# Two strips of one projection that take their weight groups in turns

## The chip, the cores and the metric

The kernel runs on one core of one Trainium2 chip. The metric is the device time of one execution in microseconds (us); the kernel before takes 2448.28 us, the median of three runs. Five engines work side by side, each through its own list of instructions in order: TensorE (PE, matrix products; PEld are its weight loads), VectorE (DVE), ScalarE (ACT), GpSimd (POOL) and SyncE (SP, which issues most of the DMAs). An instruction that must wait for another engine holds up all that stand behind it in its own list.

## The reference

Two layers work on 256 tokens of 2048 features, in float32. The even layer matters here:

```
h = rms_norm(x, g)
p = h @ w_in                      # 2048 x 4384: u | r k v | three low ranks
y_s5 = s5_mixer(u, ...)           # complex state space, 64 groups of 16 channels
y_rw = rwkv7_mixer(r, k, v, ...)  # 16 heads, a 64 x 64 state each
x = x + rms_norm(concat(y_s5, y_rw) @ w_out, g2)
x = x + rms_norm(swiglu(rms_norm(x, g3)), g4)
```

The odd layer has a gated linear recurrence in place of the two mixers, and a swiglu of the same size.

## The kernel before

**The weight stream.** Features lie on partitions, tokens on the free axis. Every projection is cut into *strips* of up to 512 output columns. A strip is fed by *groups* of weights: one group is 256 rows of the weights, [128, 2, 512] in float32. A group comes by DMA (`raw`), is split into a high part (`hi`, on ScalarE) and a low part (`lo`, on VectorE, raw minus hi), and TensorE then makes 24 products with it: 2 tiles of rows, 4 tiles of columns, and three products for each (hi by x high, hi by x low, lo by x high; lines 513 to 515). `raw`, `hi` and `lo` have three buffers each, so a group can only be split when the third group before it has been used up. Four accumulators of a strip fill two PSUM banks; two strips can have theirs at a time. In the profile the accumulators are `psw`.

**The order.** `Lanes` (lines 173 to 207) decides in what order instructions are written: the weight stream goes on, and work beside it stands in generators, one at a time in a lane, each of which is taken a step further when a clock that the program itself keeps says that its inputs are there. On the chip that order is fixed. What TensorE does for the two mixers thus stands between the groups of the stream, at places that were chosen when the program was written out.

**The opening.** The first two strips are the two halves of u, `w_u[0]` and `w_u[1]`, 8 groups each. The first one also makes its own input: `h_before(g)` scales and splits two more tiles of x (`hh` on ScalarE, line 136; `hl` on VectorE, line 131) ahead of a group, `h_behind(g)` squares tiles (`sqs`) for the norm. The sums of squares give 1 / rms (`rs`, a chain of nine small VectorE instructions, then `rstdp` on TensorE, then `rstd`). When a strip is through, `u_evac` multiplies its PSUM by that and copies it by quarters into `U` (16 copies on ScalarE, 16 on VectorE).

**S5.** Its parameters are made on VectorE (`params`), then GpSimd and VectorE make matrices for eight pieces e = 0 to 7 (`wb`, `cb`), TensorE transposes and multiplies them (`tp`, `kt`, `tm`), and `main(e)` goes: `bu` (TensorE, from `U` and `wts`), about 14 VectorE instructions with two scans, `py` (TensorE). Pieces 0 to 3 need the first half of u, 4 to 7 the second.

**RWKV.** After u come `w_lr` and eight strips of r, k, v (`w_p`), whose evacuation `elem(p)` makes the inputs of four sets of heads. When S5 is done, `solve(hf)` runs for hf = 0 to 3, one after the other in one lane: `qp` on TensorE, copies, two trips through DRAM, and 31 steps on GpSimd. `chunks(hf)`, in another lane, follows each with transposes (`vt`, `bt`, `at`), products, and four chunks of the state (`st`, `sa`, `yp`), then `norm` (`yc` on VectorE, `tp`, `gp` on TensorE, `yl`, `yrf`).

**The end of it.** The output projection takes the S5 half first (`w_eo[0]`), then two strips of the RWKV half up to their third group. There all mixer lanes are drained (`L.drain("el", "qa", "qb", "gn")`, line 1577). The fourth groups, `e0.go(3)` and `e1.go(3)`, need the last head set, split into `yrh` and `yrl`. From there on, through both swiglus and the odd layer, nearly all of the time is weight stream.

Of the kernel before, what the change touches and what calls it, by code (L numbers as in the profile page):

```python
# [19 lines left out]
T = 256  # L20
D = 2048
# [46 lines left out]
def build(tc, a, out):  # L68
# [10 lines left out]
    # An estimate of when each engine is free and each tile is written, in us: it decides the  # L79
    # order in which instructions are emitted, nothing else.  # L80
# [44 lines left out]
    def pick(n, *aps, bias=1.0):  # L125
        """VectorE or Pool, whichever is through with n elements first; VectorE never waits."""
        v, t = max(clk["V"], L.now), dep(*aps)
        return V if t < v + 0.2 and v + bias + 0.00104 * n < max(clk["G"], L.now, t) + 0.0021 * n else G
# [44 lines left out]
    class Lanes:  # L173
        """The order of emission: what runs beside the weight stream is generators, one at a
        time in each lane, that yield how many us their next step should wait for. `now`
        counts TensorE's time."""
# [41 lines left out]
    with ctx:  # L218
# [17 lines left out]
        # ---------------------------------------------------------------- small helpers  # L236
# [38 lines left out]
        def rsqrt(o, x, shape, nm):  # L275
            """o = x ** -0.5 for a few columns: an integer first guess, two Newton steps (the
            first with its constants fitted to the guess)."""
# [40 lines left out]
        def together(*gs):  # L318
            """The steps of several generators, in turns."""
            gs = list(gs)  # L320
            while gs:
                for g in list(gs):
                    if next(g, 0) == 0:
                        gs.remove(g)
                    else:
                        yield

        # rstd of each token, in every partition (in PSUM), from the sums of squares
        def keep_warm(n):
            """TensorE's clock halves when it idles for some us: products of ones that nobody  # L330
            reads, where it would wait."""
# [22 lines left out]
        class Ssq:  # L354
            """Sums over the features of the squares, plus D eps: a column for each half of the
            tokens. Squares add up by pairs of tiles before TensorE sums over the partitions."""
# [15 lines left out]
            def place(self, sums=1):  # L372
                """Where the next pair of squares goes; the first ones are the sums."""
# [18 lines left out]
        # ---------------------------------------------------------------- weight stream  # L392
        RAW, HL = [3], [3]   # how far ahead
        groups = []          # (dram, k group), in the order of use
# [3 lines left out]
        # the tiles of the stream; a second pool takes every fourth one after the even layer  # L398
# [40 lines left out]
        unread = []          # of each strip, whether its PSUM has still to be read  # L439

        class Banks:
            """Four tiles of PSUM in two banks, which are read on their own; the last tile may have
            one more bank for itself."""
# [16 lines left out]
        class Strip:  # L460
            """w [kg, 128, 2, W] in DRAM; x(k): (hi, lo) [128, T] of a k tile; the n tiles
            accumulate side by side in two PSUM banks. evac(ps) may return a generator; `lazy`
            says that it reads PSUM there. hook(g) comes before a group; mid makes the tiles of x:
            mid[0](g) comes before the split of a group, mid[1](g) after it."""
# [62 lines left out]
            def tail(self):  # L527
                """The last two groups, one PSUM bank after the other."""
# [25 lines left out]

        W4 = [P] * 4

        def of2(z):
            """k -> (hi, lo) of a tensor kept as two slots of eight tiles, hi and lo."""
# [5 lines left out]
        # the whole weight stream, in its order  # L564
# [10 lines left out]

        def plan_ffn(l):
# [3 lines left out]
        plan(*w_u, w_lr, *w_p, *w_glu, *w_eo[0], (w_eo[1][0], range(3)), (w_eo[1][1], range(3)),  # L580
# [9 lines left out]
        # ================================================================ even layer  # L590
        even = ExitStack()
        with even:
# [11 lines left out]
            # ---- S5: parameters  # L604
# [36 lines left out]
            def wrap_small(o, x, n):  # L641
                """As wrap, for up to 64 turns; two steps on ScalarE."""
# [10 lines left out]
            def params():  # L653
                """A = exp(lam dt), its powers (apw: of 4 down to 0), gamma = (A - 1) / lam, and
                the size and the angle of A^4."""
# [37 lines left out]
                def powers():  # L693
                    for s, w, t in ((3, 1, 2), (2, 2, 0)):
                        # A^2 from A, then A^3 and A^4 from A^2
# [51 lines left out]
            # ---- the norm of x: its scale goes into the split, 1 / rms into what is read of PSUM  # L747
# [53 lines left out]
            def normed(ps):  # L801
                """What a strip has in PSUM, times 1 / rms of each token."""
# [14 lines left out]
            # ---- S5, four pairs of groups at a time: q says which 32 rows of a 128-row tile, s  # L817
            # which four tiles. Blocks of four steps: row (lag, channel), column (pair, block).
# [25 lines left out]
            def s5_gen():  # L844
# [14 lines left out]
                def prep_b(e):  # L859
                    """B scaled, times the powers of A: the matrix of the input, by lag; the real  # L860
                    part of C A^j, and minus its imaginary part."""
# [7 lines left out]
                def prep_w(e):  # L869
# [12 lines left out]
                    # the response at lags 0 to 3, as a block of a Toeplitz matrix  # L882
# [974 lines left out]
def pack(inp):  # L1857
    f = np.ascontiguousarray
    g = {k: np.asarray(v) for k, v in inp.items()}
    o = {}  # L1860
# [82 lines left out]
```

## Time and profile before

| | |
|---|---|
| median of three runs | 2448.28 us (2446.85, 2448.28, 2451.95) |
| the profiled execution, its span from first to last instruction | 2446.8 us (no other time is given for it) |
| TensorE busy | 2373.5 us, 97% |
| VectorE, ScalarE, GpSimd busy | 1469.4, 1181.0, 411.8 us |
| granted TensorE clock, mean | 0.983 |
| DMA | 404 MB, 165 GB/s over the span |

Matmuls are pipelined: a busy TensorE may still run at half its clock or wait inside. "Granted clock" is the share of the full 2.4 GHz; 0.5 of it is the lower level, 1.2 GHz. "Main products" below are those of the weight stream (lines 513 to 515).

### The profile page before, as it was taken

To read this page: it belongs to the slowest core of one execution; us is meant where nothing else is said; L and a number is where in the kernel's file an instruction comes from. 1 tells how busy PE (TensorE), PEld (TensorE's weight loads), DVE (VectorE), ACT (ScalarE), POOL (GpSimd) and SP (SyncE) were. 2 spreads that over 40 slices of the span, in tenths; PEclk is the share of its full clock that TensorE was granted. 3 is DMA by queue.
4 is the path that set the end of the run, shared out by engine and by line. 5 is a ranking of instruction groups with operands and counts; after the bars stand their busy time and mean duration, and the time that the engine had idled before them with its cause. 6 is when DMAs were issued, how large, how long until landed. Compare 5 with 4: busy or idle time off the path is not lost.

```text
span 2446.8 us, 47370 instructions
## 1 busy us (share of the span) xinstructions
PE 2373.5 (97%) x19830; PEld 2328.5 (95%) x19830; DVE 1469.4 (60%) x2002; ACT 1181.0 (48%) x1550; POOL 411.8 (17%) x589
## 2 busy tenths in 40 slices
PE   7889999999999999999999999999999999999997
PEld 7888988998999999999999899998999999999997
DVE  8777667558655544555544877757555544555544
ACT  5547555545444434434433588845444444444443
POOL 4753666506000000000000400014000000000002
PEclk8888999999999999999999999999999999999999
DMA  5122543444555555555555455554555555555553
GB/s 198 58 71 73 156 123 113 143 141 164 186 185 182 185 186 184 182 186 183 183 187 181 139 181 188 175 197 138 183 185 186 182 187 183 183 186 183 182 186 116
DMA packets 127446, 404.21 MB, mean 165 GB/s; under 512 B 26112, under 2 KB 26880, under 8 KB 127104
## 3 DMA queue, kind: packets, MB, share of 16 engines
q1 hardware_dynamic: 126912, 399.61, 48.6%
q8 instruction: 155, 2.54, 0.4%
q0 software_dynamic: 320, 1.58, 0.2%
q14 instruction: 59, 0.48, 0.1%
HBM read 397.98 MB, written 3.15 MB: 164 GB/s over the span
## 4 chain that ended last, share of the span: by engine, by line
PE 73%; DVE 3%; POOL 1%; ACT 1%; issue 1%; POOLq 0%; ACTq 0%; DVEq 0%
PE psw L513 24%; PE psw L515 24%; PE psw L514 24%; DVE lo L112 1%; DVE xl L131 1%; POOL xr L112 1%; ACT hi L136 0%; PE ssq L263 0%; PE warm L263 0%; PE own L515 0%; PE own L514 0%; PE own L513 0%; POOL sqs L112 0%; DVE sqs L112 0%; POOL tg L112 0%
## 5 line engine op out<-in xcount | busy, mean ns | idle before, releaser
L112 DVE TENSOR_TENSOR lo<-raw,hi 128x1024 fp32r<-128x1024 f32 (+1 forms) x760 | 930.8, 1229 | 864.8 <-ACT hi L136 860.5
L136 ACT ACTIVATE hi<-raw 128x1024 fp32r<-128x1024 f32 (+1 forms) x760 | 783.7, 1035 | 938.6 <-PE psw L514 738.4
L514 PE MATMUL psw<-xl,hi 128*128 128x256 f32 x3328 | 942.2, 283 | 15.1 <-DVE xl L131 14.8
L513 PE MATMUL psw<-xh,hi 128*128 128x256 f32 x3328 | 941.4, 283 | 0.9 <-ACT xh L136 0.9
L515 PE MATMUL psw<-xh,lo 128*128 128x256 f32 x3328 | 940.3, 283 | 0.0
L514 PEld LDWEIGHTS psw<-xl,hi 128*128 128x128 f32 x3328 | 635.2, 191 | 19.8 <-DVE xl L131 19.8
L513 PEld LDWEIGHTS psw<-xh,hi 128*128 128x128 f32 x3328 | 635.3, 191 | 1.5 <-ACT xh L136 1.5
L515 PEld LDWEIGHTS psw<-xh,lo 128*128 128x128 f32 x3328 | 635.5, 191 | 0.0
L515 PE MATMUL psw<-hhi,lo 128*128 128x256 f32 x1364 | 384.4, 282 | 0.0
L513 PE MATMUL psw<-hhi,hi 128*128 128x256 f32 x1364 | 384.3, 282 | 0.0
L514 PE MATMUL psw<-hlo,hi 128*128 128x256 f32 x1364 | 383.8, 281 | 0.0
L112 POOL TENSOR_TENSOR sqs<-sqs 128x512 f32<-128x512 f32 x44 | 73.1, 1661 | 1518.8 <-ACT sqs L136 1518.4
L515 PEld LDWEIGHTS psw<-hhi,lo 128*128 128x128 f32 x1364 | 257.7, 189 | 0.0
L514 PEld LDWEIGHTS psw<-hlo,hi 128*128 128x128 f32 x1364 | 257.7, 189 | 0.0
L513 PEld LDWEIGHTS psw<-hhi,hi 128*128 128x128 f32 x1364 | 257.7, 189 | 0.0
L513 PE MATMUL psw<-hh,hi 128*128 128x256 f32 x560 | 175.8, 314 | 2.7 <-ACT hh L136 1.4
L514 PE MATMUL psw<-hl,hi 128*128 128x256 f32 x560 | 165.5, 296 | 5.3 <-DVE hl L131 5.3
L515 PE MATMUL psw<-hh,lo 128*128 128x256 f32 x560 | 165.6, 296 | 4.2 <-DVE lo L112 4.2
L513 PEld LDWEIGHTS psw<-hh,hi 128*128 128x128 f32 x560 | 112.8, 202 | 10.5 <-issue 5.6
L514 PEld LDWEIGHTS psw<-hl,hi 128*128 128x128 f32 x560 | 113.0, 202 | 6.2 <-DVE hl L131 5.9
L515 PEld LDWEIGHTS psw<-hh,lo 128*128 128x128 f32 x560 | 112.6, 201 | 5.8 <-DVE lo L112 5.6
L136 ACT ACTIVATE ga<-ga 128x512 f32<-128x512 f32 x52 | 32.9, 632 | 83.0 <-DVE ga L112 82.9
(426 smaller groups left out, 2760.6 us busy)
## 6 DMA issues: line engine op xcount, KB each, us to landing
raw<-in_w_fg SPq DMA_DIRECT2D x352, 512.0 KB, 3.5
raw<-in_w_fd SPq DMA_DIRECT2D x176, 512.0 KB, 3.5
raw<-in_w_oi SPq DMA_DIRECT2D x64, 512.0 KB, 3.9
raw<-in_w_p SPq DMA_DIRECT2D x64, 384.0 KB, 3.2
raw<-in_w_eo SPq DMA_DIRECT2D x32, 512.0 KB, 3.6
raw<-in_w_oo SPq DMA_DIRECT2D x32, 512.0 KB, 4.1
raw<-in_w_u SPq DMA_DIRECT2D x16, 512.0 KB, 4.0
raw<-in_w_glu SPq DMA_DIRECT2D x8, 512.0 KB, 3.5
```

The lines of the kernel that those rows point to most:

```text
L112: e.tensor_tensor(o, x, y, op=op)
L131: e.scalar_tensor_tensor(o, x, s, y, op0=op0, op1=op1)
L136: S.activation(o, x, f, bias=bias, scale=scale)
L513: TE.matmul(o, hi[:, kk, sl], xh, start=st, stop=False, skip_group_check=True)
L514: TE.matmul(o, hi[:, kk, sl], xl, start=False, stop=False, skip_group_check=True)
L515: TE.matmul(o, lo[:, kk, sl], xh, start=False, stop=en, skip_group_check=True)
```

## The change

The two strips of u are both opened at the start, and a table says which takes its next group. `plan_two` puts the groups into the weight stream in the same order. The first strip still makes the tiles of x, at the same groups of its own; the second reads the same tiles. A second edit lets `solve(2)` and `solve(3)` begin only when `chunks(0)` and `chunks(1)` have been written out to the end. Comments and docstrings are gone as well, which moves line numbers by up to 15 and does nothing else.

```diff
+        def strips_in_turns(a, b):
+            for z, g in TURNS:
+                (a, b)[z].go(g)
...
+        TURNS = [(0, 0), (1, 0), (0, 1), (1, 1), (0, 2), (1, 2), (0, 3), (1, 3), (0, 4), (0, 5), (1, 4),
+                 (0, 6), (1, 5), (0, 7), (1, 6), (1, 7)]
+
+        def plan_two(a, b):
+            for z, g in TURNS:
+                plan(((a, b)[z], range(g, g + 1)))
...
-        plan(*w_u, w_lr, *w_p, *w_glu, *w_eo[0], (w_eo[1][0], range(3)), (w_eo[1][1], range(3)),
+        plan_two(*w_u)
+        plan(w_lr, *w_p, *w_glu, *w_eo[0], (w_eo[1][0], range(3)), (w_eo[1][1], range(3)),
              (w_eo[1][0], range(3, 4)), (w_eo[1][1], range(3, 4)), *w_eo[1][2:])
...
-            vdone, ndone = set(), set()
+            vdone, ndone, cdone = set(), set(), set()
...
-                while "ready" not in H:
+                while "ready" not in H or hf > 1 and hf - 2 not in cdone:
                     yield 0.5
...
                     L.add("gn", norm(hf, c2, yc, ys, vr, rs))
+                cdone.add(hf)
...
-            strip(w_u[0], hx, W4, u_evac(0), mid=(h_before, h_behind, hat.get))
-            strip(w_u[1], hx, W4, u_evac(1))
+            strips_in_turns(Strip(w_u[0], hx, W4, u_evac(0), mid=(h_before, h_behind, hat.get)),
+                            Strip(w_u[1], hx, W4, u_evac(1)))
```

**ScalarE near the start.** These are its rows from the first four tiles of x on (`hh`: a tile's high part; `hi`: a weight group's; `sqs`: squares). Before:

```order
L136 ACTIVATE hh_118<-x0a,vec 128x256 x4
L136 ACTIVATE hi<-raw 128x1024
L136 ACTIVATE sqs<-x0a 128x512 x2
L136 ACTIVATE hh_118<-x0a,vec 128x256 x2
L136 ACTIVATE hi<-raw 128x1024
L136 ACTIVATE sqs<-x0a 128x512 x2
L136 ACTIVATE sqs<-x0b 128x512 x2
L136 ACTIVATE hh_118<-x0a,vec 128x256 x2
L136 ACTIVATE hi<-raw 128x1024
L136 ACTIVATE sqs<-x0b 128x512 x2
L136 ACTIVATE hh_119<-x0b,vec 128x256 x2
```

Now:

```order
L136 ACTIVATE hh_118<-x0a,vec 128x256 x4
L136 ACTIVATE hi<-raw 128x1024
L136 ACTIVATE sqs<-x0a 128x512 x2
L136 ACTIVATE hi<-raw 128x1024
L136 ACTIVATE hh_118<-x0a,vec 128x256 x2
L136 ACTIVATE hi<-raw 128x1024
L136 ACTIVATE sqs<-x0a 128x512 x2
L136 ACTIVATE sqs<-x0b 128x512 x2
L136 ACTIVATE hi<-raw 128x1024
```

Tiles 4 and 5 now stand behind three weight groups instead of two, and tiles 6 and 7 come further down: between two pairs of tiles stand two weight groups.

**ScalarE where u is copied out of PSUM.** `U` are the copies, `rstd` the reciprocal rms, `wts`, `kt`, `Tm` are S5 matrices. Before, from the minus sign of a parameter (`bb`) on:

```order
L136 ACTIVATE hi<-raw 128x1024
L136 ACTIVATE bb<-bb 128x512
L136 ACTIVATE hi<-raw 128x1024
L136 ACTIVATE rstd<-rstdp 128x256
L136 ACTIVATE U_175<-psw_223 32x128 x4
L136 ACTIVATE U_176<-psw_223 32x128 x4
L136 ACTIVATE U_177<-psw_223 32x128 x4
L136 ACTIVATE U_178<-psw_223 32x128 x4
L136 ACTIVATE hi<-raw 128x1024 x2
L136 ACTIVATE nn<-ang,cc__106 128x256
```

Now, from `rstd` on:

```order
L136 ACTIVATE rstd<-rstdp 128x256
L136 ACTIVATE hi<-raw 128x1024
L136 ACTIVATE wts<-tp 128x512 x2
L136 ACTIVATE kt<-kt 128x96
L136 ACTIVATE hi<-raw 128x1024
L136 ACTIVATE st<-ang 128x256
L136 ACTIVATE ct<-ang 128x256
L136 ACTIVATE ct<-ct 128x256
L136 ACTIVATE Tm_192<-tm 128x512
L136 ACTIVATE wts<-tp 128x512 x2
L136 ACTIVATE U_175<-psw_223 32x128 x4
L136 ACTIVATE U_176<-psw_223 32x128 x4
```

The first half of u was copied out before the split of the last six groups of the second half; now its copies stand behind the split of all 16 groups, and behind the transposed matrices of the first two S5 pieces.

**TensorE where the mixer lanes are drained.** `tp` and `gp` are the last head set's norm, `ssq` the first instruction after the drain. Before:

```order
L515 MATMUL psw_6487<-yrh,lo 128x256
L270 MATMUL tp<-cst,yc 128x128 x2
L513 MATMUL psw_6487<-yrh,hi 128x256
L514 MATMUL psw_6487<-yrl,hi 128x256
L515 MATMUL psw_6487<-yrh,lo 128x256
L513 MATMUL psw_6488<-yrh,hi 128x256
L514 MATMUL psw_6488<-yrl,hi 128x256
L515 MATMUL psw_6488<-yrh,lo 128x256
L263 MATMUL gp<-sg,g_6300 128x128 x4
L513 MATMUL psw_6488<-yrh,hi 128x256
L514 MATMUL psw_6488<-yrl,hi 128x256
```

Now:

```order
L513 MATMUL psw_6446<-yrh,hi 128x256
L514 MATMUL psw_6446<-yrl,hi 128x256
L515 MATMUL psw_6446<-yrh,lo 128x256
L270 MATMUL tp<-cst,yc 128x128 x2
L263 MATMUL gp<-sg,g_6374 128x128 x4
L263 MATMUL ssq<-ones 128x1 x2
L513 MATMUL psw_6254<-yrh,hi 128x256
L514 MATMUL psw_6254<-yrl,hi 128x256
```

Before, six main products stood between `tp` and `gp`, and 15 between `gp` and `ssq`; now there are none. Between the last `yp` and that `tp` stood 72, and now 36. Counted in main products from the start, the first `bu` stood behind 306 and now stands behind 360, the last `bu` behind 828 and now behind 885, the first `qp` of `solve(2)` behind 1512 and now behind 1626. The drain is at 2400 in both, and all of TensorE's rows after it are the same.

## Rows read from the trace of the kernel before

**Rows 1.** The page's busy time of TensorE, its share and instructions.
```profile
PE 2373.5 (97%) x19830; PEld 2328.5 (95%) x19830; DVE 1469.4 (60%) x2002; ACT 1181.0 (48%) x1550; POOL 411.8 (17%) x589
```
**Rows 2.** Windows of the span: length, busy us of each engine, granted clock, DMA.
```profile
core 0: us, PE busy (x) PEld busy (x) DVE busy (x) ACT busy (x) POOL busy (x), PEclk, DMA share, GB/s
16.40:47.00 30.60, 23.50 (x177) 22.69 (x177) 27.44 (x85) 14.03 (x25) 6.45 (x9) 0.94 0.54 189
47.00:77.00 30.00, 23.76 (x170) 21.91 (x169) 24.01 (x40) 15.66 (x35) 26.39 (x27) 0.79 0.26 81
77.00:247.70 170.70, 152.88 (x1110) 143.71 (x1107) 131.45 (x241) 99.23 (x179) 93.59 (x120) 0.85 0.21 66
247.70:543.30 295.60, 291.39 (x2719) 265.75 (x2718) 188.26 (x396) 154.37 (x272) 148.95 (x318) 1.00 0.44 133
700.00:900.00 200.00, 200.00 (x1678) 200.00 (x1677) 103.64 (x98) 82.52 (x86) 0.00 (x0) 1.00 0.54 185
```
**Rows 3.** Waits of TensorE, 0 to 77 us: total, times, longest.
```profile
PE psw L514 <- DVE hl L131: 5.3, 2, 3.3
PE tm L270 <- DVE kt L131: 3.6, 1, 3.6
PE psw L515 <- DVE lo L112: 3.0, 2, 2.2
PE rstdp L263 <- DVE rs L131: 2.9, 1, 2.9
...
PE psw L513 <- ACT hi L136: 1.1, 1, 1.1
```
**Rows 4.** Waits of TensorE, 247 to 544 us, the first and the last.
```profile
PE bp L263 <- DVE av L131: 1.4, 1, 1.4
...
PE kn L263 <- ACT esq L136: 0.7, 1, 0.7
```
**Rows 5.** Timeline of TensorE at four places: start, length, operation, idle before.
```profile
11.48 0.58 PE L514 MATMUL psw<-hl,hi 128*128 128x256 f32 x1 [3.29 <-DVE hl L131]
...
16.50 0.28 PE L513 MATMUL psw<-hh,hi 128*128 128x256 f32 x1
...
19.37 0.28 PE L513 MATMUL psw<-hh,hi 128*128 128x256 f32 x1
...
76.95 2.42 PE L263 MATMUL bu<-U,wts 128*128 128x64 f32 x16
...
360.64 1.16 PE L263 MATMUL qp<-ar,bk 64*128 64x128 f32 x16
```
**Rows 6.** Timeline of VectorE, ScalarE and GpSimd, 12 to 51 us.
```profile
12.53 1.21 DVE L112 TENSOR_TENSOR lo<-raw,hi 128x1024 fp32r<-128x1024 f32 x1
...
42.12 1.42 DVE L112 TENSOR_TENSOR m<-y,bb 128x256 f32<-128x256 f32 x4
...
44.09 2.46 POOL L112 TENSOR_TENSOR m<-y,bb 128x256 f32<-128x256 f32 x4 [19.30 <-DVE bb L112]
...
46.22 0.35 DVE L131 SCALAR_TENSOR_TENSOR rs<-trm,rs 128x2 f32<-128x2 f32 x1
...
47.71 1.76 DVE L112 TENSOR_TENSOR lo<-raw,hi 128x1024 fp32r<-128x1024 f32 x1
...
50.11 4.46 ACT L136 ACTIVATE U<-psw 32x128 f32<-32x128 f32 x16 [2.30 <-DVE psw L112]
```
**Rows 7.** Timeline of TensorE and VectorE at the last state chunk, 529 to 544.
```profile
529.47 0.40 PE L263 MATMUL yp<-sav,q 128*64 128x64 f32 x4
...
536.77 0.42 DVE L112 TENSOR_TENSOR yc<-yc,gr 128x256 f32<-128x256 f32 x1
...
538.54 0.38 PE L270 MATMUL tp<-cst,yc 128*128 128x128 f32 x2
...
539.47 1.63 PE L263 MATMUL gp<-sg,g 128*128 128x128 f32 x8
...
542.28 0.76 DVE L112 TENSOR_TENSOR yrl<-yrf,yrh 128x256 fp32r<-128x256 f32 x2 [0.48 <-ACT yrh L136]
```

## The prediction

> **What bounds the kernel now.** I read the page first. TensorE is busy 97% of the span [rows 1], so a gain can only come from time in which TensorE waits or runs at half its clock. The windows show where that is. Between 700 and 900 us it is busy all the time at the full clock, 1678 products in 200 us [rows 2]: nothing is to be had there, and the change does not touch it. From 247.7 to 543.3 it still runs at 1.00 and is busy 291.4 of 295.6 us [rows 2]; its waits there are four, from 1.4 to 0.7 us, 3.8 us in all [rows 4]. Before 247.7 it is different: the granted clock averages 0.94, 0.79 and 0.85 in the three windows, and TensorE is idle 7 us, 6 us and 18 us of them [rows 2]. The change starts in the first two of these windows. There the waits show that TensorE waits for tiles of x (`hl`), for low parts of weights (`lo`), for the norm (`rs`) and for S5 matrices (`kt`) [rows 3]: it is fed too late, by VectorE and ScalarE.
>
> A group of weights at the full clock lasts 2.87 us, from 16.50 to 19.37 [rows 5], so a main product costs 0.1196 us. That is the unit below.
>
> **The change, part by part.** No arithmetic is added or removed. What moves is when TensorE gets which work. I follow the program to three points: the first `bu`, the drain, and the end.
>
> *To the first `bu`.* Before, it starts at 76.95 [rows 5]. Now 54 more main products stand ahead of it (360 instead of 306): +6.5 us. Against that, these waits go:
> - the second wait for `hl`, 2.0 us (5.3 less 3.3 for the very first tile, which stays [rows 3]): a pair of tiles now serves two groups, and has 5.7 us of products to be made behind, not 2.9;
> - the waits for `lo`, 3.0 us [rows 3]: VectorE has the tiles of one pair and two groups to prepare in 5.7 us, not the tiles and one group in 2.9; one `lo` is 1.21 us, or 1.76 beside GpSimd [rows 6];
> - the wait of `rstdp` for `rs`, 2.9 us [rows 3]: the first strip had run out before the norm was ready. Now 264 main products stand ahead of `rstdp` instead of 192;
> - 1.1 us for `hi` [rows 3]: ScalarE's copies of u, 4.46 us [rows 6], stood ahead of splits; now they stand behind all of them;
> - 3.6 us for `kt` before `tm` [rows 3]: seven VectorE instructions stood between a split and that copy, some with matrices from GpSimd as inputs; now four do. I count it as gone; it may stay whole.
>
> That is 12.6 us. Two new waits come. The split of the twelfth group now stands behind VectorE's block of parameter products and `rs`, from 42.12 to 46.57, 4.45 us [rows 6], with TensorE still in the strips: between 0 and 4.45, I take 2.2. And the first `kt` is reached sooner, while GpSimd's chain, which starts at 44.09 [rows 6], starts no sooner: VectorE's products, on which it waits, stand behind two more splits (+2.4) and two pairs of tiles fewer (-1.6). I take 1.5, between 0 and the 3.6 that a late S5 matrix cost before [rows 3]. Last, the clock: at 0.94 over 30.6 us and 0.79 over 30.0 us it costs 1.8 and 6.3 us of work [rows 2], and its fall goes with the waits there. With 3.7 us of waits in place of 12.6 I take back 5 of these 8.1, between 0 and 8.1. The first `bu` then starts at 76.95 + 6.5 - 12.6 + 3.7 - 5.0 = 69.6, which is **7.4 us sooner**, with more of the stream done.
>
> What covered the copies of u is thinner: 24 main products and two `kt` stand between the end of the first strip and `bu`, some 3.5 us; the first quarter needs two multiplications of PSUM and eight copies, four on each engine, a quarter of the 4.46 us on ScalarE and about as much before it. This fits if VectorE is free, and costs 1 to 2 us if not; it is in the range.
>
> *S5.* From the first `bu` to the last, TensorE has 522 main products before and 525 now. The copies of the second half lie inside this stretch in both orders. I take it as equally long; its 18 us of idle and its clock of 0.85 [rows 2] say that it could move by 4 us either way.
>
> *To the drain.* It stands at 2400 main products in both. The 54 that were done early are missing now: **-6.5 us**. But the mixer's chain ends later in the stream. Before, the last `yp` ends at 529.87 and the last head set's `yc` is ready at 537.19 [rows 7], 7.3 us later; 72 main products, 8.6 us, lay over it. Now 36 do, 4.3 us: a wait of 3.0. Then from `tp` at 538.54 to the first half of `yrl` at 542.66 are 4.1 us [rows 7]; before, main products filled them, now only `tp` and `gp`, 2.1 us: a wait of 2.0. Together **+5.0**. Between the first `qp` and here the chain has 1452 main products beside it instead of 1509, 6.8 us less cover; I add **+2** for smaller waits (0 to 4: before, four waits cost 3.8 [rows 4]).
>
> *`solve(2)`.* Its new condition costs nothing by itself: what waits is the writing of the program. The price is where its work lands: the rival of the rigid chain.
>
> *The sum.* -7.4 - 6.5 + 5.0 + 2.0 = -6.9 us, on the profiled execution's span of 2446.8: 2439.9. The median of the runs shown is 1.5 above that span, so I forecast **2441.4 us**.
>
> **The rivals.**
>
> *S5's preparation sets the first `bu`.* GpSimd's chain to it lasts from 44.09 to 76.95 [rows 5, 6], 32.9 us. If that is rigid, `bu` comes at 77.7 (GpSimd starts 0.8 later by the count above), and the sum is +0.8 - 6.5 + 7.0 = +1.3: 2449.6; half rigid gives 2445.5. For it: GpSimd is busy 26.4 of the 30 us after 47 [rows 2]. Against it: TensorE waited only 3.6 us for VectorE's `kt` there, and 2.9, 1.1 and 2.0 for other things. It may also gain from the splits: a `lo` took 1.76 us beside GpSimd and 1.21 alone [rows 6], and five splits of the u strips follow the start of GpSimd's chain in the new order, 2.7 us at that difference.
>
> *The clock stays down.* If the smaller waits that remain still hold the clock at a mean of 0.94 and 0.79 in these windows [rows 2], the 5 us are not given back, and the sum is -1.9: 2446.4. For it: the new order still leaves some 3.7 us of waits. Against it: from 16.50 to 19.37, right behind a group at half speed, a group already ran at 2.87 us [rows 5], so the clock rises soon where TensorE is fed. One rule speaks against the change here. The Trainium skill (TensorE: Matmul & The Clock Gate, Loop structure matters more than you think) advises to finish all the rows of one output before the next one begins, since the matmuls then follow each other and stay at the high clock; the new order gives that up. By that rule nothing is taken back, which is this rival. The trace speaks against it: before, the first strip followed that advice and had 0.94 [rows 2], and what broke it were waits for tiles and splits, which come less often when a tile serves two outputs.
>
> *The chain from `solve(2)` on is rigid: slower.* Its `qp` at 360.64 [rows 5] starts what ends with the last `gp` at 541.10 [rows 7], 180.5 us. `qp` now stands 114 main products later, 13.6 us. TensorE arrives earlier by what it saved up to there, 7.4 + 6.5 = 13.9 by my sum. If nothing in the chain can shrink, the drain comes 0.3 us sooner: 2448. If the opening saves only half, 7 us, it comes 6.6 us later: **2455**. It decides from a saving under 8.7 us. For it: the solves stand in one lane, and each has two trips through DRAM. Against it: TensorE waited only 3.8 us in 296 [rows 4], so most steps had been ready before it came; the last `yc` was ready 1.35 us before its `tp` [rows 7].
>
> *More than forecast.* If the clock comes back whole (3 more), the new waits do not appear (3.7 more) and the small ones neither (2), it is 2432.7. For it speaks that VectorE and ScalarE idle in these windows too [rows 2]; against it that GpSimd does not.
>
> **How the numbers follow.** Forecast, 0.48, with a range of its own from 2435 to 2447; more than forecast, 0.14; S5's preparation, 0.14; the clock, 0.06; rigid chain, 0.18, of it 0.13 slower and 0.05 no change. What a measurement here can tell is about 0.2%, 4.9 us: faster means under 2443.4. The forecast gives 0.46 to faster and 0.02 to no change. So faster 0.46 + 0.14 = 0.60, the same 0.02 + 0.14 + 0.06 + 0.05 = 0.27, slower 0.13. The range, 2431 to 2451, takes in the first two rivals whole and the better half of the third, and leaves out 0.1 to 0.2.
>
> **What the profile will show.** Right: the clock in 16 to 47 us near 1.00, no wait of 2 us or more for `hl`, `lo` or `rs` after the first group; the first `bu` at 65 to 73; the last `bu` sooner by about as much; TensorE idle some 5 us in two pieces just before the drain; everything behind the drain as long as before. Wrong: `bu` at 75 or later with waits for `kt`, `tm` or `tp` ahead of it (first rival); waits of TensorE for `q`, `ft` or `st` of several us each between 360 and 540, against 3.8 in all now (third); a clock of 0.8 in both windows with few waits (second); or S5 longer by more than 4 us, for which I have no term.

## The result: slower by 0.51%, and the profile after

The changed kernel takes 2459.06 us (median of five runs, 2455.66 to 2464.81), the kernel before 2448.28 on the same chip (2446.85 to 2452.68). The ratio is 1.0051, with a 95% interval from 1.0039 to 1.0064: **slower by some 12 us** (10.8 by the two medians), where 2441.4 was forecast and nothing above 2451 was in the range. The profiled execution has a span of 2457.3 us, 10.5 more than before.

The windows of the changed kernel, against [rows 2] (length, busy us of each engine, granted clock, DMA):

```profile
16.40:47.00 30.60, 29.87 (x248) 29.67 (x248) 27.42 (x78) 19.54 (x31) 10.36 (x10) 1.00 0.66 226
47.00:77.00 30.00, 22.24 (x159) 20.11 (x158) 23.14 (x35) 10.22 (x24) 24.66 (x27) 0.77 0.22 66
77.00:251.40 174.40, 155.30 (x1103) 145.44 (x1102) 133.27 (x258) 106.96 (x193) 91.68 (x116) 0.82 0.23 69
251.40:552.00 300.60, 288.80 (x2661) 262.49 (x2660) 184.90 (x387) 148.63 (x264) 147.04 (x320) 0.98 0.42 126
700.00:900.00 200.00, 200.00 (x1677) 200.00 (x1677) 103.66 (x98) 81.95 (x87) 0.00 (x0) 1.00 0.55 184
```

The first row is what the change was forecast to do: 29.87 us busy of 30.60 at the full clock, against 23.50 at 0.94 before. The second row shows nothing of it: TensorE idles 7.8 us of the 30, before it was 6.2. The third is 3.7 us longer than before, and in the fourth TensorE is busy 288.8 of 300.6 us where it was busy 291.4 of 295.6. The last row is as before.

TensorE's waits, first from 0 to 77 us, against [rows 3]:

```profile
PE psw L514 <- DVE hl L131: 4.9, 2, 3.6
PE psw L515 <- DVE lo L112: 2.0, 1, 2.0
PE kt L263 <- POOL cb L112: 1.9, 1, 1.9
PE kt L263 <- DVE cb L112: 1.5, 1, 1.5
...
PE rstdp L263 <- DVE rs L131: 0.7, 1, 0.7
PE tm L270 <- DVE kt L131: 0.6, 1, 0.6
```

and from 251 to 552 us, against [rows 4]:

```profile
PE bp L263 <- DVE av L131: 2.9, 3, 1.0
PE psw L515 <- DVE lo L112: 2.6, 3, 1.5
PE tp L270 <- DVE yc L112: 1.9, 1, 1.9
PE wa L263 <- ACT sav L136: 1.7, 1, 1.7
```

The waits for `rs` and for `kt` before `tm` went as forecast, but the S5 matrices (`cb`) take their place. Between 251 and 552 there are now eleven waits where there were four.

The timeline of TensorE at the places of [rows 5] and [rows 7]:

```profile
76.25 1.97 PE L263 MATMUL bu<-U,wts 128*128 128x64 f32 x16 [0.41 <-DVE U L148]
...
378.14 1.16 PE L263 MATMUL qp<-ar,bk 64*128 64x128 f32 x16
...
548.39 0.41 PE L270 MATMUL tp<-cst,yc 128*128 128x128 f32 x2 [1.88 <-DVE yc L112]
548.63 2.50 PE L263 MATMUL gp<-sg,g 128*128 128x128 f32 x8
551.06 1.01 PE L263 MATMUL ssq<-ones 128*128 128x1 f32 x4
```

The first `bu` comes 0.7 us sooner, `solve(2)`'s `qp` 17.5 us later, the last `tp` 9.9 later.

Four points of the program divide the loss: the first `bu`, the first `qp` (where `solve(0)` begins), the `ssq` right behind the drain, and the `ssq` that has 2862 main products ahead of it. From that last one to the end, each of the kernels below needs 1833 us. The times are from the timelines of the profiled executions; "ahead" is the number of main products ahead of the first `qp`.

| kernel | ratio to before, 95% | first bu | first qp | ahead | qp to drain | drain to ssq 2862 |
|---|---|---|---|---|---|---|
| before | 1 | 77.0 | 247.7 | 891 | 295.2 | 70.6 |
| changed | 1.0051 (1.0039 to 1.0064) | 76.2 | 251.4 | 948 | 299.7 | 72.9 |
| e1, wait alone | 1.0016 (1.0007 to 1.0024) | 75.2 | 243.4 | 891 | 297.9 | 71.5 |
| e2, changed, u with two products | 1.0066 (1.0053 to 1.0079) | 77.9 | 248.9 | 948 | 308.0 | 73.9 |
| e3, changed, products of ones before py | 1.0041 (1.0026 to 1.0056) | 76.5 | 248.1 | 948 | 297.9 | 73.2 |
| e4, changed, py by input | 1.0038 (1.0026 to 1.0050) | 76.6 | 243.8 | 948 | 308.5 | 73.9 |
| e5, changed, 6.5 us held | 1.0007 (0.9998 to 1.0016) | 77.5 | 245.8 | 891 | 301.3 | 73.0 |
| e6, before, u with two products | 1.0002 (0.9993 to 1.0011) | 76.1 | 247.0 | 891 | 294.9 | 70.4 |
| e7, before, py by input | 0.9976 (0.9966 to 0.9985) | 75.7 | 239.2 | 891 | 295.1 | 70.4 |
| e8, e5 and py by input | 1.0002 (0.9994 to 1.0011) | 76.9 | 243.6 | 891 | 297.5 | 72.9 |
| e9, e5 without the wait | 0.9994 (0.9985 to 1.0003) | 77.8 | 244.6 | 891 | 295.0 | 70.4 |
| e10, e9 and py by input | 0.9983 (0.9974 to 0.9992) | 77.2 | 241.9 | 891 | 295.0 | 70.4 |
| e11, changed, pair 5 held | 1.0056 (1.0043 to 1.0068) | 76.2 | 251.3 | 948 | 303.3 | 72.4 |
| e12, changed, pair 5 held less | 1.0059 (1.0046 to 1.0073) | 77.6 | 247.2 | 948 | 302.9 | 73.4 |
| e13, changed, 5.0 us held | 1.0110 (1.0094 to 1.0125) | 76.5 | 255.7 | 945 | 300.9 | 74.0 |
| e14, changed, 2.5 us held | 1.0064 (1.0051 to 1.0077) | 77.5 | 252.2 | 924 | 300.8 | 71.6 |

(In e2 and e6 128 of the products "ahead" are left out. The profiled execution is one of several: in e2, e4 and e5 it took 3.4, 6.7 and 4.8 us more than the median of the runs, in e1, e14 and e13 2.9, 2.7 and 7.9 us less, in the others less than 1.6 us more or less. The stages of those six are to be read with that in mind; the ratios are taken over all runs.)

For the changed kernel this adds up: -0.7 to the first `bu`, +4.4 from there to the first `qp` (175.15 for 170.74), +4.4 to the drain, +2.3 behind it: 10.4.

Two things are to be read in this table. The first `bu` comes at 75.2 to 77.9 us in all sixteen, whatever TensorE has to do before it. In the five kernels whose order from the first `qp` on is that of before without the wait on `chunks` (before, e6, e7, e9, e10), `qp` to drain is 294.9 to 295.2 and the next stretch 70.4 to 70.6: what is won ahead of the first `qp` there is kept whole. In all the others these two stretches are together 3.6 to 16.6 us longer than before, though eight of them have 33 to 57 main products (4 to 6.8 us) fewer beside the chain.

### The profile page after: what moved, and what is told of

The parts are those of the page before. It is cut to its first block, busy times and chain, and to the rows that moved or that the text cites. A ratio compares the mean times of both kernels' runs of the same rounds, so it can differ in the third digit from the quotient of the medians.

```text
span 2457.3 us, 47364 instructions
## 1 busy us (share of the span) xinstructions
PE 2380.1 (97%) x19830; PEld 2333.8 (95%) x19830; DVE 1464.9 (60%) x2004; ACT 1183.6 (48%) x1551; POOL 407.1 (17%) x587
## 4 chain that ended last, share of the span: by engine, by line
PE 83%; DVE 8%; ACT 2%; POOL 2%; issue 2%; DMA 1%; SPq 0%; POOLq 0%; ACTq 0%; DVEq 0%
PE psw L513 26%; PE psw L515 26%; PE psw L514 26%; DVE lo L112 2%; DVE m L112 1%; DVE xl L131 1%; ACT hi L136 1%; PE py L263 1%; PE yp L263 1%; POOL sq L112 1%; PE gp L263 1%; PE bu L263 1%; POOL lf L112 0%; DVE m L152 0%; DMA lm<-mtd 0%
```

## The experiments

**e1: the wait alone.** The kernel before with the second edit:

```diff
-                while "ready" not in H:
+                while "ready" not in H or hf > 1 and hf - 2 not in cdone:
...
+                cdone.add(hf)
```

> The kernel before with one of the two edits: solve(hf) for hf over 1 waits until chunks(hf - 2) is written out; the two u strips run one after the other as before. Up to the second qp the order is that of the kernel before; solve(2) has 6 main products more ahead of it, solve(3) 24, and the last tp, which had 21 main products behind it, has none. Theory A (the strips in turns cannot move the S5 preparation, the products done early are lost later, and the end of the mixer loses its cover): only the end is touched here, 1.9 us of wait and about 2 us at half speed, 2449 to 2453 us. Theory B (the wait on chunks makes the loss, by holding back the chain of solves): most of the 10.8 us is here, 2456 to 2460. Theory C (TensorE's granted clock in the S5 stage makes the loss): that stage has no changed instruction here, so its half-speed pieces are those of before and the time is 2447 to 2451.

Measured: 1.0016, some 4 us, of the three expectations A's: 2450.92 also lies at the end of C's range, but the kernel before took 2446.70 in this comparison, and 4.2 us more are the upper end of A's and beyond C's. The price is not where I put it, at the tail: the last `tp` waits for nothing. `solve(3)`'s `qp` now comes right behind the last `yp` of `chunks(1)`; the substitution of `solve(2)` on GpSimd, which it follows in its lane, had long ended. GpSimd in this kernel, then TensorE:

```profile
408.76 0.21 POOL L112 TENSOR_TENSOR sq<-lf,lm 128x8 f32<-128x8 f32 x1
```
```profile
426.56 0.40 PE L263 MATMUL yp<-sav,q 128*64 128x64 f32 x4
...
428.14 1.16 PE L263 MATMUL qp<-ar,bk 64*128 64x128 f32 x16
```

From the last step of the substitution to the `qp` are 19.4 us. Before, they were 9.2:

```profile
416.64 0.20 POOL L112 TENSOR_TENSOR sq<-lf,lm 128x8 f32<-128x8 f32 x1
```
```profile
425.81 1.16 PE L263 MATMUL qp<-ar,bk 64*128 64x128 f32 x16
```

TensorE loses time there in one place: at 421.89 the product `bp` waits 1.73 us for `yl`, and the granted clock is 0.83 from 420 to 430 us. Before, TensorE is busy without a break at 1.00 from 364 us to this `qp`.

**e2 and e6: TensorE's work in the opening taken away.** The third product of the u strips is left out, in the changed kernel and in the one before:

```diff
-                        TE.matmul(o, hi[:, kk, sl], xl, start=False, stop=False, skip_group_check=True)
-                        TE.matmul(o, lo[:, kk, sl], xh, start=False, stop=en, skip_group_check=True)
+                        TE.matmul(o, hi[:, kk, sl], xl, start=False, stop=en and self.w in w_u, skip_group_check=True)
+                        if self.w not in w_u:
+                            TE.matmul(o, lo[:, kk, sl], xh, start=False, stop=en, skip_group_check=True)
```

> The changed kernel without the third product (low half of the weights by high half of x) in the two u strips, so u is less exact: 128 main products fewer, 15.3 us at 0.1196 us each; nothing else moves in the order. Theory A: VectorE and GpSimd set when the first bu can start; it stays at 74 to 77 us, TensorE waits longer ahead of it (at kt, tm or bu), and the whole is 2455 to 2462 us. Rival (TensorE's main products, through the end of strip 0 and its U, set the first bu in the changed kernel): the first bu at 62 to 68 us, and 2444 to 2451 us.

> The kernel before without the third product (low half of the weights by high half of x) in the two u strips, so u is less exact: 128 main products, 15.3 us at full clock, taken from TensorE ahead of the S5 stage; nothing else moves in the order. Theory A (VectorE, GpSimd and ScalarE set when S5 starts and how long it takes): the first bu stays at 75 to 79 us, TensorE waits longer ahead of it, and the whole is within 4 us of before, 2443 to 2452. Rival (the opening is TensorE's, and time won there is kept): 2432 to 2437.

Measured: nothing is gained by 15.3 us less work, 1.0066 and 1.0002 (2462.47, half a us above A's range, as the first `bu` is 0.9 us above it, and 2448.19, inside it). The first `bu` in e2, behind a wait for GpSimd's matrix, and in e6:

```profile
76.99 0.43 PE L263 MATMUL kt<-wb,cb 128*32 128x128 f32 x8 [1.60 <-POOL cb L112]
77.86 2.36 PE L263 MATMUL bu<-U,wts 128*128 128x64 f32 x16 [0.44 <-DVE U L148]
```
```profile
71.98 1.12 PE L270 MATMUL tm<-cst,kt 128*128 128x128 f32 x4 [3.20 <-DVE kt L131]
...
76.06 2.00 PE L263 MATMUL bu<-U,wts 128*128 128x64 f32 x16
```

This settles the opening: TensorE does not set the first `bu`; VectorE and GpSimd do, and TensorE only waits longer when it has less to do. How rigid their chain is shows in all sixteen kernels: the first `bu` follows the first of GpSimd's products, `m`, by 31.9 to 32.9 us, wherever between 42.8 and 45.8 us that one starts. Before, it starts at 44.09 [rows 6]; in the changed kernel and in e2:

```profile
44.14 2.47 POOL L112 TENSOR_TENSOR m<-y,bb 128x256 f32<-128x256 f32 x4 [12.41 <-DVE bb L112]
```
```profile
45.79 2.46 POOL L112 TENSOR_TENSOR m<-y,bb 128x256 f32<-128x256 f32 x4 [13.12 <-DVE bb L112]
```

**e3 and e4: the half speed and the waits for `spi` in the S5 stage.** e3 puts six unread products ahead of each `py` group; e4 orders its twelve products by input:

```diff
-                    for i in range(4):
-                        o = py[:, 64 * i:64 * i + 64]
-                        mm(o, Tm..., U[:, i, :], stop=False)
-                        mm(o, cb[e % 2][0]..., spr[:, i, :], start=False, stop=False)
-                        mm(o, cb[e % 2][1]..., spi[:, i, :], start=False)
+                    for i in range(4):
+                        mm(py[:, 64 * i:64 * i + 64], Tm..., U[:, i, :], start=i == 0, stop=False, ...)
+                    for z, x in enumerate((spr, spi)):
+                        for i in range(4):
+                            mm(py[:, 64 * i:64 * i + 64], cb[e % 2][z]..., x[:, i, :], start=False, ...)
```

> The changed kernel with six products of ones that nobody reads (128x128, about 0.22 us apart) ahead of each of the eight py groups, where TensorE waits for spi (6 waits, 8.0 us in all); the order is otherwise the same. Theory C: with TensorE kept at work in these waits the half-speed pieces after them go (S5 stage from 76 to 238 us at 0.81 of the clock now, to over 0.9), and the time falls by 4 to 10 us, to 2449 to 2455. Theory A with VectorE as the pace of the S5 stage: the products fill waits and displace nothing, 2457 to 2462. If the waits are shorter than the products (1.3 us) once the clock is up, up to 5 us are added: 2464.

> The changed kernel with the twelve products of a py group in another order: the four of U, the four of spr, then the four of spi (before, the third product of the group was already one of spi). Eight products, some 1.7 us, can run ahead of spi instead of two. The six spi waits (8.0 us) should fall to under 2 us in all. If idle TensorE time and the half speed after it set the S5 stage's length: 5 to 9 us sooner at the first qp (251.4 now) and 2450 to 2455 us. If the chain on VectorE and GpSimd sets it: the products wait elsewhere, qp within 2 us of 251.4, and 2457 to 2461.

Measured: from the first `bu` to the first `qp`, the changed kernel, e3 and e4 in this order:

```profile
76.20:251.40 175.20, 156.05 (x1108) 146.22 (x1108) 134.05 (x260) 107.72 (x196) 92.48 (x117) 0.82 0.23 68
```
```profile
76.50:248.10 171.60, 156.17 (x1204) 147.19 (x1204) 137.36 (x260) 107.41 (x196) 94.34 (x117) 0.89 0.24 71
```
```profile
76.60:243.80 167.20, 142.91 (x1110) 132.48 (x1110) 135.28 (x259) 107.67 (x197) 95.93 (x119) 0.91 0.24 71
```

The waits for `spi` fall from 8.0 us to 3.0 and 1.7, the clock rises from 0.82 to 0.89 and 0.91, and the stage is 3.6 and 8.0 us shorter. That is what theory C expects of this stage, but single executions show it weakly: e11 and e12 below, which have the changed kernel's order up to the first `qp`, took 175.2 us at 0.83 and 169.6 at 0.85, so 3.6 us are not clear of noise. The medians, 2454.3 and 2454.5, are at the upper end of its ranges, but before took 2446.7 in the same comparison; by the ratios the kernels are 0.10% and 0.13% under the change, with overlapping intervals. In e4's profiled execution, the slowest of its five, the gain is lost again behind the first `qp`: 308.5 us to the drain. By the ratios the clock in S5 accounts for a fifth to a quarter of the loss, if for any.

**e5 and e9: the lead taken out of the order.** Both are the changed kernel with

```diff
+            L.now += 6.5
             strip(w_lr, hx, [P, P, 32], lr_evac)
```

e9 also drops the wait on `chunks`, which this order does not need.

> The changed kernel with 6.5 us added to the program's own clock behind the u strips (one line), so that the main products run no longer ahead of the side work in the order. From the fourth bu on, every side product has as many main products ahead of it as in the kernel with the wait on chunks alone (bu 513 to 828, first qp 891, third qp 1518, fourth 1842, last tp 2400); only the opening is that of the changed kernel. Theory A now reads: the chain of S5 and of the solves sets the pace; with 54 to 120 main products more ahead of it, the strips end sooner against it, their evacuations and the elementwise work of the pairs stand ahead of S5's steps on VectorE and GpSimd, and TensorE waits for the chain. Then this kernel gives the time of the wait alone, 2449 to 2453 us: first bu at 76 to 77, last bu 228 to 233, third qp 357 to 363. Rival (the opening's 8 us are kept once the order is right): 2440 to 2446. Rival (it is the turns' opening itself, not the order behind it, that makes the S5 stage slow): 2456 to 2460.

> The u strips in turns, with 6.5 us added to the program's own clock behind them and without the wait of solve(hf) on chunks(hf - 2): from the fourth bu to the drain every side product has as many main products ahead of it as in the kernel before (third qp 1512, fourth 1818, last tp 2379); only the opening is changed. This is the edit with the turns by itself, its lead taken out of the order. Theory A (the opening's TensorE time is worth nothing, the chain sets the pace): 2444 to 2450 us, within 4 us of before, last bu 228 to 234. Rival (the opening's 8 us are kept when nothing else changes): 2437 to 2442.

Measured: 1.0007 and 0.9994 (2450.21 and 2445.77, both inside theory A's ranges). With the side work where the kernel before has it, the loss is gone, 0.44% of 0.51%. With the wait gone too, the turns by themselves cannot be told from no change. So the opening, in which TensorE loses 7.8 us less (from 16.4 to 47.0 us, 30.60 - 23.50 x 0.94 = 8.5 before and 30.60 - 29.87 = 0.7 now), is worth nothing that these runs can tell (e9's interval allows 0.15%), though e9 has it too: 30.10 us busy of 30.60 at 0.99. The loss comes from what the two edits do to the order behind it.

**e7, e8 and e10: `py` by input in orders that hold.**

> The kernel before with the twelve products of each of the eight py groups in the order U, spr, spi, so that eight of them and not two can run ahead of spi; the order is otherwise the same. In the changed kernel this made the S5 stage 7.6 us shorter (first qp 243.8 for 251.4) but the solves lost it again, TensorE's main products there being late. Theory A: in this order, where the solves' side products have fewer main products ahead of them, S5 ends 4 to 8 us sooner (first qp 240 to 244), and as TensorE is busy without a wait from there to the drain, half to all of it stays: 2440 to 2446. Rival (all is lost again, as in the changed kernel): 2446 to 2450.

> The changed kernel with both edits: 6.5 us on the program's own clock behind the u strips, and the py products by input. If the two add up as theory A has it, S5's last bu at 222 to 229 and first qp at 238 to 243, 2443 to 2449 us; the tail's wait at the drain (no main product behind the last tp) stays at 1 to 3 us. If the py order's gain is lost in the solves as in the changed kernel: 2449 to 2454.

> The same with the py products by input (U, spr, spi), against the kernel before with that order alone (ratio 0.9976). Theory A: the turns add nothing to it, 2438 to 2445 us. Rival (the opening is worth something once S5's steps are not held by spi): 2432 to 2437.

Measured: 0.9976, 1.0002 and 0.9983. In time e7 and e10 are inside theory A's ranges; e8, 2449.05, is on the border of its two. Against the same kernel without the new order of `py`, e8 and e10 are 0.05% and 0.11% under e5 and e9, with overlapping intervals: the gain is clear only in the order of before. e7 beats both kernels by the most: 2441.22 us, with none of the change in it. Its windows from the first `bu` to the first `qp` and on to the drain, and those of the kernel before:

```profile
75.70:239.20 163.50, 145.60 (x1109) 136.43 (x1105) 132.01 (x241) 98.96 (x179) 97.02 (x120) 0.88 0.23 69
239.20:534.30 295.10, 290.78 (x2714) 265.27 (x2714) 187.19 (x396) 154.07 (x272) 148.95 (x318) 1.00 0.44 132
```
```profile
77.00:247.70 170.70, 152.88 (x1110) 143.71 (x1107) 131.45 (x241) 99.23 (x179) 93.59 (x120) 0.85 0.21 66
247.70:542.90 295.20, 290.99 (x2714) 265.35 (x2714) 188.12 (x396) 153.97 (x272) 148.95 (x318) 1.00 0.44 132
```

TensorE's idle time in the S5 stage is the same (17.9 and 17.8 us); the 7.2 us come from fewer busy microseconds, 145.6 for 152.9, at a higher clock. And here they stay.

**e11 and e12: one place in the solves.** In the changed kernel the sixth pair's GpSimd products stand inside the substitution of `solve(1)`. GpSimd in the kernel before, first and last step and what follows:

```profile
319.22 0.66 POOL L112 TENSOR_TENSOR sq<-lf,lm 128x31 f32<-128x31 f32 x1 [1.34 <-DMA lm<-mtd]
...
347.97 0.80 POOL L112 TENSOR_TENSOR sq<-lf,lm 128x8 f32<-128x8 f32 x1
351.44 1.58 POOL L112 TENSOR_TENSOR yl<-yl,bv 128x128 f32<-128x128 f32 x2 [2.12 <-ACT yl L136]
...
354.93 0.74 POOL L112 TENSOR_TENSOR rk<-rk,av 128x256 f32<-128x256 f32 x1 [1.86 <-DVE av L120]
```

and in the changed kernel:

```profile
329.02 0.24 POOL L112 TENSOR_TENSOR sq<-lf,lm 128x31 f32<-128x31 f32 x1 [1.24 <-DMA lm<-mtd]
...
348.64 0.73 POOL L112 TENSOR_TENSOR rk<-rk,av 128x256 f32<-128x256 f32 x1 [4.22 <-DVE av L120]
...
366.71 1.30 POOL L112 TENSOR_TENSOR yl<-yl,bv 128x128 f32<-128x128 f32 x2 [3.01 <-ACT yl L136]
...
369.83 0.20 POOL L112 TENSOR_TENSOR sq<-lf,lm 128x8 f32<-128x8 f32 x1
```

`rk` and `yl`, which came behind it, now stand in it with their waits: 40.8 us instead of 28.8. It is 39.7 to 40.9 in e2, e3 and e4 too, and 28.8 to 29.5 in e1, e5, e7 and e9. The edit holds them back:

```diff
-                    while p >= 4 and (p // 2 - 2) not in vdone:
+                    while p >= 4 and (p // 2 - 2) not in vdone or p == 5 and "sub" not in HV[1]:
...
+                    if s == 23:            # e12: s == 19
+                        H["sub"] = True
```

> The changed kernel with one hold more in the program: the elementwise work of the sixth pair of heads (its GpSimd products rk, bk, ar) is written only when the substitution of solve(1) on GpSimd is at its 24th of 31 steps, so that these products stand behind it, as they do in the kernel before; now they stand inside it. In the changed kernel this substitution takes 40.8 us (329.0 to 369.8), in the kernel before 28.8. solve(2) then has 1593 main products ahead of it (1626), solve(3) as many as now (1938), the last tp too (2400). Theory A (GpSimd's queue makes the late half of the loss): the substitution takes 30 to 34 us, the third qp comes at 367 to 372 us instead of 378.1, and as solve(3) keeps its place only part of it reaches the end: 2452 to 2458. Rival (the substitution has slack; the loss is made in the S5 stage and by TensorE's clock): third qp at 374 to 378, 2457 to 2461.

> The same hold released at the 20th step: one of the pair's three GpSimd products still stands inside the substitution, the two others behind it; third qp behind 1596 main products, fourth behind 1896 instead of 1938, the last tp but one behind 2370 instead of 2340, the last behind 2400. Theory A: substitution 30 to 36 us, third qp at 367 to 373, fourth at 432 to 442 instead of 446.9; the drain is held by the norm's tail as now; 2450 to 2457 us. Rival as above: 2457 to 2461.

Measured: the substitution falls to 33.9 and 33.6 us and the third `qp` comes at 371.9 and 366.8, as theory A had it, and the time does not move: 1.0056 and 1.0059, as the rival had it. The part of theory A that named this place as the cause has fallen. In e11 the fourth `qp` comes at 448.4 (446.9 in the changed kernel): it stands behind the end of `chunks(1)` as before the mend. In e12 the fourth comes at 439.7, 7.2 us sooner, and still the drain is reached at 550.1, where the changed kernel has 551.1. What one place gives back is lost again further on.

**e13 and e14: smaller holds**, 5.0 and 2.5 us in place of 6.5.

> The changed kernel with 5.0 us (not 6.5) added to the program's own clock behind the u strips. The S5 steps stand earlier (bu 360, 423, 477, 573, 624, 678, 729, 819 for 360, 453, 513, 612, 675, 771, 828, 885), but from the second qp on each side product has as many main products ahead of it as in the changed kernel (1338, 1626, 1938, last tp 2400). If the loss is made in the solves (a sixth pair's products inside the second substitution on GpSimd, and the fourth solve behind chunks(1)): the last bu comes at 226 to 234, the second substitution takes 39 to 42 us, and the end is that of the changed kernel, 2455 to 2461 us. If it is made in the S5 stage: 2448 to 2453.

> The same with 2.5 us: bu 360, 444, 495, 564, 621, 681, 729, 822; first qp 924 (948 in the changed kernel, 891 in that with 6.5), second 1302, third 1548, fourth 1842, last tp 2400; from the fourth qp on the order is that of the wait alone. If the solves' order makes the loss: near the wait alone and the 6.5 us, 2447 to 2454 us. If the opening S5 steps do (second bu still behind 444 main products): last bu at 234 to 240, 2454 to 2461.

Measured: 1.0110 and 1.0064, above all the ranges given. e13's last `bu` comes at 231.8 as expected, 5.9 us before that of the changed kernel, and its substitution takes 41.0; but its first `qp`, with 126 main products between the two, comes at 255.7. e14's last `bu` comes at 229.2, sooner than its second expectation had it, and its time is no better for it. So here an early S5 gave nothing back where the solves stand late; why e13 is 0.6% worse than the changed kernel is not shown. And the loss does not grow with the lead: 0, 2.5, 5.0 and 6.5 us of hold give +0.51, +0.64, +1.10 and +0.07%. It is not the lead as such that costs but the order that the program writes for it.

## Why the prediction was wrong

**The step that failed** is "To the first `bu`": I summed TensorE's waits there as if their going brought `bu` nearer, -7.4 us. Measured: -0.7 (76.95 to 76.25). I had the other case as a rival, GpSimd's chain as rigid, at 0.14. The evidence that I held against it, that TensorE waited only 3.6 us for `kt`, was no evidence: an engine that arrives late at a rigid chain waits little for it. What decided was in [rows 2]: GpSimd busy 26.4 of 30 us. GpSimd's chain did not start 0.8 us later, as I had counted, but at 44.14 (44.09 before), and `bu` came 32.1 us behind it (32.9).

**"The 54 that were done early are missing now: -6.5"** failed with it, and more dearly. It takes the stretch to the drain as TensorE's. From the first `qp` to the drain the changed kernel has 57 main products fewer beside the chain, and takes 299.7 us where it took 295.2. So the rival of the rigid chain, which also gave the nearest time (2455), had the right kind of cause, though not its numbers: I put its start at `solve(2)` and a saving of 8.7 us as its point of decision. From `solve(2)`'s `qp` to the end of the last `gp` are now 173.0 us (378.14 to 551.13), not the 180.5 of before [rows 5, 7]; it shrank by 7.5 of the 17.5 us that `qp` came later.

**"I take it as equally long"**, S5 from the first `bu` to the last, by 4 us either way: first to last `bu` start 161.5 us for 154.5, but 155.9 in e12, in the same order, so that most of the 7.0 us may be this execution's. One place shows how the new order can cost time. VectorE and TensorE of the changed kernel, ahead of the second `bu`:

```profile
95.31 1.65 DVE L112 TENSOR_TENSOR lo<-raw,hi 128x576 fp32r<-128x576 f32 x2
101.06 0.76 DVE L112 TENSOR_TENSOR lo<-raw,hi 128x576 fp32r<-128x576 f32 x1 [4.10 <-ACT hi L136]
...
108.26 0.41 DVE L112 TENSOR_TENSOR m<-ct,bu 128x256 f32<-128x256 f32 x1
```
```profile
95.11 0.58 PE L513 MATMUL psw<-hh,hi 128*128 128x256 f32 x1 [3.73 <-ACT hi L136]
...
98.44 0.41 PE L515 MATMUL psw<-hh,lo 128*128 128x256 f32 x1
...
102.02 0.28 PE L515 MATMUL psw<-hh,lo 128*128 128x256 f32 x1
...
104.70 1.90 PE L263 MATMUL bu<-U,wts 128*128 128x64 f32 x16
```

93 main products now stand between the first two `bu`, 63 before; they wait for a split (3.73 us) and then run at the lower clock (granted 0.50 from 96 to 101 us), 0.41 us each for 0.28. In e5, with 36 between them, VectorE has the second `bu` ten microseconds sooner:

```profile
98.05 0.42 DVE L112 TENSOR_TENSOR m<-ct,bu 128x256 f32<-128x256 f32 x1
```

Most of this is made up by the third `bu` (121.4 for 121.1). How much of the 4.4 us between the first `bu` and the first `qp` is the order's I can't say: e11 and e12, the same order up to there, took 175.2 and 169.6.

**"`solve(2)`: its new condition costs nothing by itself."** It costs 0.16% alone (e1), with the wait of 1.73 us and the half speed ahead of `solve(3)`, which I did not look at; between e9 and e5 it is 0.13%, with overlapping intervals.

**The tail**, +5.0: 1.9 us of wait at the last `tp`, and 2.3 us more from the drain to the `ssq` behind 2862 products, where the clock is 0.97 for 1.00 and where I had expected no change. The size was about right. The +2 for small waits was too little: TensorE's idle time from the first `qp` to the drain grew from 4.2 us (295.20 less 290.99) to 11.8 (300.60 less 288.80), of which the tail's wait is 1.9, and some half speed came with it, a granted clock of 0.98 for 1.00 over these windows.

**Right** were the opening up to 47 us (16 to 47 at 1.00; the wait for `rs` 0.7 us for 2.9, `kt` before `tm` 0.6 for 3.6, `hi` and the old waits for `lo` and the second `hl` gone) and, of the signs named ahead, "`bu` at 75 or later" and "S5 longer by more than 4 us". The new waits that I had counted came, and were larger: at the twelfth group 3.3 us (1.3 for `hl` at 48.78, 2.0 for `lo` at 51.20) where I took 2.2, and at the first `kt` 3.4 (`cb`) where I took 1.5. A slip without consequence: six VectorE instructions, not seven, stood between the split and the copy `kt`.

**The rule that I weighed against the change.** From 16.4 to 47.0 us two outputs in turns ran at 1.00. In the Trainium skill (TensorE: Matmul & The Clock Gate, Loop structure matters more than you think) the good loop nest does finish one output before the next, but what the section sets against it as bad is a long wait for a DMA between the matmuls, not two outputs in turns. The new order gives up the form of the good nest and brings nothing of the bad one.

**What stays open:** which of the displaced steps costs how much. The orders differ in many places, and mending one did not move the time. The turns with neither the wait nor the hold were not run, so what each of the two edits costs in the changed kernel's own order is not told apart; e1 gives the wait's price in the order of before alone.

## What to carry to other kernels

Before pricing a wait of the busiest engine, ask who is late: if the chain that it waits for has its own work and no slack, the wait is only moved, and work taken off the busy engine there is worth nothing; leaving out 15.3 us of it is a cheap test. Where a program's own clock places the side work, a few microseconds gained at the front re-deal the whole order behind, so hold the clock back to separate the edit from its new order. And a group of products that needs a late input is best written with all that does not need it first: that alone was worth 0.24% in the kernel before; in three other orders it was 0.05 to 0.13%, which is not clear of noise.

## What the runs showed of the hardware

In the S5 stage idle time is not all that waits cost. In e7 TensorE's idle time there is that of the kernel before (17.9 and 17.8 us), yet the stage is 7.2 us shorter at a clock of 0.88 for 0.85. In e3 48 products of ones lift the clock from 0.82 to 0.89; the 3.6 us by which the stage is shorter there are less than the 5.6 us between two executions in one order (e11, e12). In the changed kernel TensorE, idle for 3.73 us, runs at the lower level from 95.1 to about 101.5 us, and at 1.00 again from 102 to 105 us.
